# Products with the moving operand and the output taken backwards, and weights that begin 16 bytes further with each chunk

## The chip, the cores and the metric

The kernel runs on one core of one Trainium2 chip. The metric is the device time of one execution in microseconds. The matrix engine is called PE, its weight loads PEld, VectorE is DVE, ScalarE is ACT, GpSimd is POOL and SyncE is SP.

## The reference, cut to what matters

Two transformer blocks are computed one after the other on 256 tokens of 1,024 features (the first block also has 16 meta tokens, so that some of its products have 272 columns). All weights and inputs are float32.

```python
def first_block(...):
    h = concatenate([pad, meta, x])
    h = h + 0.5 * swiglu(rms_norm(h, ffn1_norm), ffn1_w_in, ffn1_w_out)   # 1024 -> 2 x 2816 -> 1024
    h = h + token_mixer(rms_norm(h, mix_norm), ...)                       # two attentions, gates, w_out
    h = h + 0.5 * swiglu(rms_norm(h, ffn2_norm), ffn2_w_in, ffn2_w_out)
    return h[:, BLOCK:]

def second_block(...):
    h = x + head_group_mixer(rmsnorm(x), ...)            # convolution and retention
    h = h + memory_cross_attention(rmsnorm(h), mem_n, ...)
    h = h + sq_relu_mlp(rmsnorm(h), up_w, down_w)        # 1024 -> 4096 -> 1024
    return rmsnorm(h)
```

Nearly all of the arithmetic is in the products of the activations with the weight matrices.

## The kernel before, in words

The activations stand feature-major: features on the 128 partitions, tokens along the free axis. The residual stream is `hA` and then `hB`, eight tiles of 128 features each. All weights are read once, in the order of their use, as a stream of chunks of up to 2,048 columns by 128 rows (`_plan`). `_Weights.load` brings a chunk into `raw` with a DMA of SP; `_high` lets ACT copy it, rounded to float32r, into `hi`; `piece` lets DVE put the rest, `raw - hi`, into `lo`. `raw`, `hi` and `lo` have three buffers each.

An activation is split in the same way into two float32r parts: `XH` and `XL` for the residual stream, `AHf`/`ALf` (feed-forward with a gate), `AHm`/`ALm` (last layer), `YH`/`YL`, `OFH`/`OFL`, `OS`, `CH`/`CL`, `OXH`/`OXL` and, for the memory, `MH`/`ML`, which take the place of `hA` and `BM`.

A product of a 128x128 block of weights with a tile of activations is then three matrix products in `mm3` (L501 to L504): high with high, high with low, low with high. Each loads its 128 columns of weights anew and takes 256 or 272 columns of the activation as the moving operand; all products of an output tile add up in one bank of PSUM (`ps` or `po`). For some output tiles the 272 columns are taken as two runs of 128 with the meta tokens left out (`qv`). `products_t` (L984 to L996) does the same for 512 output columns with the activation as the loaded operand and the weights as the moving one; it doesn't go through `mm3`.

The order of the work is written out by hand. `step` emits the products of a unit, then the work that follows the unit before it, then splits weights ahead. Nothing in the order of the work is touched by the change, except that four tiles of the mixers (`OFH`, `OFL`, `dec`, `krz`) are allocated earlier in their pools.

Tiles are placed in the order of their allocation, one behind the other: in `base` come `par`, `c0`, `cst`, `hA` (8 x 288 columns), `hB` (8 x 256), `XH` and `XL` (8 x 288 each), `BM` (8 x 290), `cosr`, `sinr` and small buffers; then the chunks' `raw`, `hi` and `lo`; then the pools of the layers. A column of float32 or float32r takes 4 bytes.

Of the kernel before, what the change touches and what calls it, by code (L numbers as in the profile page):

```python
# [17 lines left out]
P = 128  # L18
# [5 lines left out]
TP = 288  # L24
DFF = 2816
# [13 lines left out]
# ---------------------------------------------------------------- weight order  # L39
def _plan():  # L40
    """The order in which the weights are streamed: chunks of blocks
    (key, array, row tile, first column, columns)."""
# [79 lines left out]
    # ends[c]: the column behind the products that start in chunk c or, where  # L122
    # those of one output tile go on in the next chunk, behind that one
# [9 lines left out]
# ------------------------------------------------------- constants of the shapes  # L133
# [4 lines left out]
for _n, _w in (("id", P), ("bd", P), ("centre", P), ("ones512", P), ("swap", P), ("fmask", TP), ("vmask", 512)):  # L138
    _CST[_n] = (_CST_N, _w)
    _CST_N += _w  # L140
_OH_N = 384 + 272
# [70 lines left out]
def _pack(inp):  # L212
    """Layout only: transposes, permutes and concatenates the inputs."""
# [56 lines left out]
# -------------------------------------------------------------------- the stream  # L270
class _Weights:
    """Streams the weights through SBUF and splits each chunk exactly into two
    float32r parts, some columns ahead of the products that use it."""
# [27 lines left out]

    def _high(self, n):
        c, a = self.c, self.o
        at, size = self.start[c]
        if a == 0:
            self.hi[c] = self.pool.tile([P, CH], F32R, tag="hi", bufs=3, name=f"hi{c}")
            self.lo[c] = self.pool.tile([P, CH], F32R, tag="lo", bufs=3, name=f"lo{c}")
        b = min(a + n, size)
        self.nc.scalar.activation(self.hi[c][:, a:b], self.raw[c][:, a:b], AF.Copy)  # L309
        self.begun.append((c, a, b))  # L310
        self.c, self.o = (c + 1, 0) if b == size else (c, b)

    def piece(self, to, n=1024):
        """Splits a piece of the stream unless the split has come to column
        `to`; the high part runs a piece ahead of the low part."""
        if to is None or self.done >= to or self.done >= self.total:
            return False
        while sum(self.start[self.free]) <= self.used:
            self.free += 1
        while len(self.begun) < 2 and self.c < min(len(self.start), self.free + 3):  # L320
            self._high(n)
        c, a, b = self.begun.pop(0)
        if self.beside:
            self.beside((b - a) / 1024)
        self.nc.vector.tensor_tensor(self.lo[c][:, a:b], self.raw[c][:, a:b], self.hi[c][:, a:b].bitcast(F32),  # L325
                                     op=ALU.subtract)
        self.done = self.start[c][0] + b
        if b == self.start[c][1]:
            self.load()
        return True  # L330
# [5 lines left out]
    def span(self, key, to):  # L336
        """Of the products from `key` to `to`: the column behind them, and how
        far the split is to be while they run."""
# [17 lines left out]
class _Core:  # L356
    """What the phases share: the engines, the constants, the weight stream and
    the order of emission.  Work that follows a unit of products is a generator;
    at each yield a piece of the weights ahead is split, and at `yield LATER` the
    rest is put behind the next unit's products."""  # L360
# [28 lines left out]
    def step(self, key, mm, evac=(), hook=None, bg=1, last=False, to=None,  # L389
             ahead=True):  # L390
        """One unit of the weight stream: its products, then the work that
        follows the unit before it, then the split of weights ahead."""
# [25 lines left out]
def _program(ctx, tc, I, out, probe=None):  # L418
# [18 lines left out]
    def bank():  # L437
        """A bank of PSUM; those kept for long sums take part while `spare`."""
        turn[0] = (turn[0] + 1) % 8
        if spare[0] and turn[0] >= 5:  # L440
            return bank_o()
        return psum.tile([P, 512], F32, tag="ps", bufs=5, name=name("ps"))
# [3 lines left out]

    def tmp(pool, tag, n=TP, bufs=2, dt=F32):
        return pool.tile([P, n], dt, tag=tag, bufs=bufs, name=name(tag))
# [5 lines left out]
    # ------------------------------------------------ first loads  # L454
    par = base.tile([P, _PAR_N], F32, name="par")
    c0 = base.tile([P, _CST0_N], F32, name="c0")
    cst = base.tile([P, _CST_N], F32, name="cst")
    hA = base.tile([P, KD, TP], F32, tag="hA", name="hA")
    hB = base.tile([P, KD, SEQ], F32, name="hB")
    XH = base.tile([P, KD, TP], F32R, name="XH")  # L460
    XL = base.tile([P, KD, TP], F32R, name="XL")
    BM = base.tile([P, H, 290], F32, tag="BM", name="BM")
# [24 lines left out]
    def qv(ap):  # L487
        return ap.rearrange("p (s c) -> p s c", c=144)[:, :, :P]
# [4 lines left out]
    def backwards(ap):  # L493
        """The last axis, of P columns, backwards."""
# [5 lines left out]
    # ------------------------------------------------ pieces  # L500
    def mm3(o, w, x, start, stop):  # L501
        T.matmul(o, w[0], x[0], start=start, stop=False)  # L502
        T.matmul(o, w[0], x[1], start=False, stop=False)  # L503
        T.matmul(o, w[1], x[0], start=False, stop=stop)  # L504
# [13 lines left out]
    def squares(acc, src, m, n):  # L518
        """The square on ScalarE; returns what adds it to the sum."""
# [7 lines left out]
    def finish(hm, m, n, gain, acc, hold=None):  # L527
        """A tile of the residual stream is there: the parts that the next
        products take, with the next norm's gain, and the sum of squares, which
        can be put off with `hold`."""  # L530
# [11 lines left out]
    def rsqrt(dst, src):  # L542
        """dst = (src + eps) ** -0.5 as exp(-ln / 2)."""
# [4 lines left out]
    def rms(acc, n):  # L548
        """The row factor of a norm, the same on all partitions."""
# [15 lines left out]
    def products(tag, ms, x, evac, ks=range(KD), late=2, out=None, between=(), **kw):  # L565
        """Output tiles `ms` together: the last `late` input tiles come last, for
        all of them; evac(m, bank) follows.  between[i] is emitted behind the
        first part of tile i."""
# [15 lines left out]
    # ------------------------------------------------ feed-forward with a gate  # L584
    def ffn(f, d, n, h, gain, acc_in, acc_out, bg, together):
        with tc.tile_pool(name="ffn" + f, bufs=2, reuse_waits="tile") as pool:
            AH = pool.tile([P, MF, n], F32R, bufs=1, name="AH" + f)
            AL = pool.tile([P, MF, n], F32R, bufs=1, name="AL" + f)
# [49 lines left out]
    # ------------------------------------------------ token mixer  # L638
    def attention_head(pool, st, h, s_of, mask_of, cut):
        """The two query tiles of a head: scores, softmax, transposed rows,  # L640
        values.  Scores and mask come with the sign changed."""
# [54 lines left out]
    def attention_end(pool, st, OH, OL):  # L696
        """The meta tokens' part, of all heads at once."""
# [15 lines left out]
    def mixer(acc_in, acc_out):  # L713
        with tc.tile_pool(name="mixer", bufs=1, reuse_waits="tile") as pool:
            kz = pool.tile([P, H, T1], F32, tag="kz", name="kz")
            qz = pool.tile([P, H, SEQ], F32, tag="qz", name="qz")
            ks = pool.tile([P, 2, T1 + 1], F32, name="ks")
# [29 lines left out]
            def head_norm(x, n):  # L747
                """The squares' mean over the 64 features of each of a tile's two
                heads; what is yielded last turns it into 1 / rms."""
# [90 lines left out]
            def value(ps, dst, meta):  # L840
                """A tile of values, token-major; of the meta tokens a copy for
                each head."""
# [53 lines left out]
            OFH = pool.tile([P, 4, SEQ], F32R, name="OFH")  # L896
            OFL = pool.tile([P, 4, SEQ], F32R, name="OFL")
# [71 lines left out]
    # ------------------------------------------------ convolution and retention  # L969
# [14 lines left out]
    def products_t(tag, j, x, evac, **kw):  # L984
        """512 output columns, token-major."""
# [14 lines left out]
    def mixer2(acc_in, acc_out, MH, ML, accm, kx, vx, rm, held):  # L1000
        with tc.tile_pool(name="mixer2", bufs=1, reuse_waits="tile") as pool:
            U = pool.tile([P, 4, 30 + SEQ], F32, name="U")
            cv = pool.tile([P, 4, SEQ], F32, name="cv")
            dec = pool.tile([P, H, 384], F32, tag="dec", name="dec")
            krz = pool.tile([P, H, SEQ], F32, tag="krz", name="krz")
# [21 lines left out]
            def convolve(n):  # L1027
                """Some taps on VectorE, of two tiles in turn."""
# [100 lines left out]
            def row_factor():  # L1129
                """The norm's factor by token, on the partitions."""  # L1130
# [25 lines left out]
            # retention, with the decay as a full matrix  # L1156
# [37 lines left out]
            # group norm over each head's features  # L1194
# [32 lines left out]
            # layer norm over the channels of the convolution, while the other  # L1227
            # half of the output products runs
# [53 lines left out]
    # ------------------------------------------------ attention to the memory  # L1282
# [104 lines left out]
    # ------------------------------------------------ squared-relu layer and the last norm  # L1387
# [51 lines left out]
    # ------------------------------------------------ tables that depend on small inputs  # L1439
    def bias_strips(pool):  # L1440
        """The windowed attention's bias by distance, as a row per query; a tile's
        queries stand there, and in its scores, backwards."""
# [32 lines left out]
    def angles(pool):  # L1475
        """Cosines and sines of the rotary positions; the angles are reduced with
        2 pi in three parts and the multiple in two, so that products are exact."""
# [46 lines left out]
    # ------------------------------------------------ the whole  # L1524
# [70 lines left out]
```

## Time and profile before

| | us |
|---|---|
| median of 2 runs | 989.56 |
| lowest and highest | 989.34, 989.77 |
| span of the profiled execution | 988.1 |
| PE busy in it | 971.6 |
| DVE busy | 675.5 |
| ACT busy | 537.5 |

The span reaches from the first to the last instruction of one further, profiled execution; the runs' times also hold what lies around it. Busy time counts a stretch once, however many products overlap in it.

### The profile page before, as it was taken

To read this page: it belongs to the slowest core of one execution; us is meant where nothing else is said; L and a number is where in the kernel's file an instruction comes from. 1 tells how busy PE (TensorE), PEld (TensorE's weight loads), DVE (VectorE), ACT (ScalarE), POOL (GpSimd) and SP (SyncE) were. 2 spreads that over 40 slices of the span, in tenths; PEclk is the share of its full clock that TensorE was granted. 3 is DMA by queue.
4 is the path that set the end of the run, shared out by engine and by line. 5 is a ranking of instruction groups with operands and counts; after the bars stand their busy time and mean duration, and the time that the engine had idled before them with its cause. 6 is when DMAs were issued, how large, how long until landed. Compare 5 with 4: busy or idle time off the path is not lost.

```text
span 988.1 us, 18399 instructions
## 1 busy us (share of the span) xinstructions
PE 971.6 (98%) x7667; PEld 942.0 (95%) x7667; DVE 675.5 (68%) x1232; ACT 537.5 (54%) x927; POOL 9.9 (1%) x15
## 2 busy tenths in 40 slices
PE   7999999999999999999999999999999999999996
PEld 7999999999989899999999999889899999999996
DVE  5676556657885758677665657999976677665452
ACT  7545435447575656656454447556474566564441
POOL 0000000020000000000000000000000000000000
PEclk9999999999999999999999999999999999999998
DMA  8754527544433225555545656443543246564531
GB/s 299 225 219 175 171 88 235 186 163 162 160 101 126 94 100 213 214 209 176 194 164 169 201 183 240 167 150 135 208 166 139 89 175 226 193 209 177 175 124 43
DMA packets 31363, 169.05 MB, mean 171 GB/s; under 512 B 5144, under 2 KB 8864, under 8 KB 14640
## 3 DMA queue, kind: packets, MB, share of 16 engines
q1 hardware_dynamic: 30928, 167.34, 48.8%
q8 instruction: 60, 0.98, 0.4%
q10 hardware_dynamic: 288, 0.52, 0.1%
q14 instruction: 23, 0.19, 0.1%
q0 software_dynamic: 64, 0.01, 0.0%
HBM read 166.79 MB, written 1.07 MB: 170 GB/s over the span
## 4 chain that ended last, share of the span: by engine, by line
PE 96%; DMA 1%; DVE 1%; ACT 1%; SPq 0%; issue 0%; DVEq 0%; ACTq 0%
PE ps L502 18%; PE ps L503 18%; PE ps L504 18%; PE po L503 10%; PE po L502 10%; PE po L504 10%; PE ps L649 1%; DMA raw<-in_ws_dram 1%; PE ps L996 1%; PE ps L995 1%; PE ps L994 1%; PE po L691 1%; PE ps L1297 1%; PE ps L1163 0%; PE po L1335 0%; PE po L705 0%
## 5 line engine op out<-in xcount | busy, mean ns | idle before, releaser
L325 DVE TENSOR_TENSOR lo<-raw,hi 128x1024 fp32r<-128x1024 f32 (+2 forms) x334 | 373.2, 1129 | 50.7 <-ACT hi L309 45.6
L309 ACT ACTIVATE hi<-raw 128x1024 fp32r<-128x1024 f32 (+2 forms) x334 | 321.8, 978 | 142.6 <-issue 48.0
L502 PE MATMUL ps<-XH,hi 128*128 128x256 f32 (+2 forms) x976 | 283.6, 291 | 5.8 <-ACT hi L309 4.2
L504 PE MATMUL ps<-XH,lo 128*128 128x256 f32 (+2 forms) x976 | 277.0, 284 | 0.7 <-DVE lo L325 0.7
L503 PE MATMUL ps<-XL,hi 128*128 128x256 f32 (+2 forms) x976 | 276.9, 284 | 0.0
L502 PEld LDWEIGHTS ps<-XH,hi 128*128 128x128 f32 (+1 forms) x976 | 184.4, 189 | 8.4 <-ACT hi L309 4.2
L503 PEld LDWEIGHTS ps<-XL,hi 128*128 128x128 f32 (+1 forms) x976 | 184.9, 189 | 1.8 <-DVE XL L516 0.5
L504 PEld LDWEIGHTS ps<-XH,lo 128*128 128x128 f32 (+1 forms) x976 | 184.1, 189 | 1.3 <-DVE lo L325 0.9
L502 PE MATMUL po<-XH,hi 128*128 128x256 f32 (+1 forms) x456 | 129.8, 285 | 0.2 <-DVE br L1060 0.2
L504 PE MATMUL po<-XH,lo 128*128 128x256 f32 (+1 forms) x456 | 128.5, 282 | 0.5 <-DVE lo L325 0.5
L503 PE MATMUL po<-XL,hi 128*128 128x256 f32 (+1 forms) x456 | 128.4, 282 | 0.0
L502 PEld LDWEIGHTS po<-XH,hi 128*128 128x128 f32 x456 | 85.7, 188 | 0.6 <-DVE br L1060 0.4
L503 PEld LDWEIGHTS po<-XL,hi 128*128 128x128 f32 x456 | 86.0, 189 | 0.1
L504 PEld LDWEIGHTS po<-XH,lo 128*128 128x128 f32 x456 | 85.5, 187 | 0.7 <-DVE lo L325 0.7
L613 ACT ACTIVATE s<-gr 128x272 f32<-128x272 f32 (+1 forms) x44 | 18.7, 425 | 109.1 <-DVE gr L611 109.1
L502 PE MATMUL ps<-AHf,hi 128*128 128x272 f32 (+1 forms) x220 | 62.8, 286 | 0.0
L504 PE MATMUL ps<-AHf,lo 128*128 128x272 f32 (+1 forms) x220 | 62.8, 285 | 0.0
L503 PE MATMUL ps<-ALf,hi 128*128 128x272 f32 (+1 forms) x220 | 62.7, 285 | 0.0
L1034 DVE SCALAR_TENSOR_TENSOR cv<-U,par,cv 128x256 f32<-128x256 f32 x120 | 50.0, 473 | 0.2 <-ACT cv L1067 0.2
L611 DVE TENSOR_TENSOR gr<-ps,r 128x272 f32<-128x272 f32 (+1 forms) x28 | 12.1, 433 | 52.9 <-PE ps L504 45.6
L503 PE MATMUL ps<-ALm,hi 128*128 128x256 f32 x160 | 45.3, 283 | 0.0
L504 PE MATMUL ps<-AHm,lo 128*128 128x256 f32 x160 | 45.3, 283 | 0.0
(385 smaller groups left out, 1835.7 us busy)
## 6 DMA issues: line engine op xcount, KB each, us to landing
raw<-in_ws_dram SPq DMA_DIRECT2D x128, 1024.0 KB, 4.9
raw<-in_ws_dram SPq DMA_DIRECT2D x32, 704.0 KB, 4.2
raw<-in_ws_dram SPq DMA_DIRECT2D x3, 512.0 KB, 5.2
dec<-in_dec_dram SPq DMA_DIRECT2D x1, 1536.0 KB, 6.3
BM<-drow SPq DMA_DIRECT2D x2, 512.0 KB, 7.5
memraw<-in_mt_dram SPq DMA_DIRECT2D x1, 1024.0 KB, 6.9
hA<-in_xt_dram SPq DMA_DIRECT2D x3, 273.0 KB, 5.6
raw<-in_ws_dram SPq DMA_DIRECT2D x3, 256.0 KB, 5.7
```

The lines of the kernel that those rows point to most:

```text
L309: self.nc.scalar.activation(self.hi[c][:, a:b], self.raw[c][:, a:b], AF.Copy)
L325: self.nc.vector.tensor_tensor(self.lo[c][:, a:b], self.raw[c][:, a:b], self.hi[c][:, a:b].bitcast(F32), op=ALU.subtract)
L502: T.matmul(o, w[0], x[0], start=start, stop=False)
L503: T.matmul(o, w[0], x[1], start=False, stop=False)
L504: T.matmul(o, w[1], x[0], start=False, stop=stop)
L611: V.tensor_tensor(gr, g[:, :n], r[0][:, :n], op=ALU.mult)
L613: S.activation(s, gr, AF.Silu)
L649: T.matmul(ps[:, at : at + n], lhs, rhs, start=True, stop=True)
L691: T.matmul(o, st["v"](h, 0), pt[:, :SEQ], start=t % 2 == 0, stop=False)
L994: T.matmul(ps[i], xh[:, t], wh, start=k == 0, stop=False)
L995: T.matmul(ps[i], xl[:, t], wh, start=False, stop=False)
L1034: V.scalar_tensor_tensor(cv[:, m], U[:, m, j : j + SEQ], prm("cw", m * 31 + j), cv[:, m], op0=ALU.mult, op1=ALU.add)
```

## The change

`mm3` takes its two moving operands and its output with a step of -1 along each free axis, so that the last column goes first; column for column the same product is computed. The parts `hi` and `lo` of chunk c begin `place(c)` = 4 * (c % 16) columns, that is 16 * (c % 16) bytes, behind the start of their buffers, which are 64 columns longer. The other tiles of `base` are rounded up to multiples of 64 columns (256 bytes), the rows of `XH` and `XL` from 288 to 320 columns and those of `AHf` and `ALf` from 272 to 320. Four tiles of the mixers are allocated earlier, and the scratch of the dynamic DMAs is set to 4,096. Comments and docstrings are dropped.

```diff
+XP = 320
+LINE = 64
...
+def place(c):
+    return 4 * (c % 16)
...
+    def _part(self, tag, c):
+        t = self.pool.tile([P, CH + LINE], F32R, tag=tag, bufs=3, name=f"{tag}{c}")
+        at = place(c)
+        return t[:, at : at + CH]
+
     def _high(self, n):
...
-            self.hi[c] = self.pool.tile([P, CH], F32R, tag="hi", bufs=3, name=f"hi{c}")
-            self.lo[c] = self.pool.tile([P, CH], F32R, tag="lo", bufs=3, name=f"lo{c}")
+            self.hi[c] = self._part("hi", c)
+            self.lo[c] = self._part("lo", c)
...
     def tmp(pool, tag, n=TP, bufs=2, dt=F32):
-        return pool.tile([P, n], dt, tag=tag, bufs=bufs, name=name(tag))
+        t = pool.tile([P, -(-n // LINE) * LINE if pool is base else n], dt, tag=tag, bufs=bufs, name=name(tag))
+        return t[:, :n]
...
-    par = base.tile([P, _PAR_N], F32, name="par")
-    c0 = base.tile([P, _CST0_N], F32, name="c0")
-    cst = base.tile([P, _CST_N], F32, name="cst")
+    par = base.tile([P, 256], F32, name="par")[:, :_PAR_N]
+    c0 = base.tile([P, 192], F32, name="c0")[:, :_CST0_N]
+    cst = base.tile([P, _CST_P], F32, name="cst")[:, :_CST_N]
...
-    XH = base.tile([P, KD, TP], F32R, name="XH")
-    XL = base.tile([P, KD, TP], F32R, name="XL")
-    BM = base.tile([P, H, 290], F32, tag="BM", name="BM")
+    XH = base.tile([P, KD, XP], F32R, name="XH")
+    XL = base.tile([P, KD, XP], F32R, name="XL")
+    BM = base.tile([P, 2368], F32, tag="BM", name="BM")[:, : H * 290].rearrange("p (h n) -> p h n", h=H)
...
+    def turned(ap):
+        return ap[:, ::-1] if len(ap.shape) == 2 else ap[:, ::-1, ::-1]
+
     def mm3(o, w, x, start, stop):
-        T.matmul(o, w[0], x[0], start=start, stop=False)
-        T.matmul(o, w[0], x[1], start=False, stop=False)
-        T.matmul(o, w[1], x[0], start=False, stop=stop)
+        o, xh, xl = turned(o), turned(x[0]), turned(x[1])
+        T.matmul(o, w[0], xh, start=start, stop=False)
+        T.matmul(o, w[0], xl, start=False, stop=False)
+        T.matmul(o, w[1], xh, start=False, stop=stop)
...
-            AH = pool.tile([P, MF, n], F32R, bufs=1, name="AH" + f)
-            AL = pool.tile([P, MF, n], F32R, bufs=1, name="AL" + f)
+            AH = pool.tile([P, MF, -(-n // LINE) * LINE], F32R, bufs=1, name="AH" + f)[:, :, :n]
+            AL = pool.tile([P, MF, -(-n // LINE) * LINE], F32R, bufs=1, name="AL" + f)[:, :, :n]
```

## Rows read from the trace of the kernel before

**Rows 1.** The page's first part: span, then busy us (share) xinstructions.

```profile
span 988.1 us, 18399 instructions
...
PE 971.6 (98%) x7667; PEld 942.0 (95%) x7667; DVE 675.5 (68%) x1232; ACT 537.5 (54%) x927; POOL 9.9 (1%) x15
```

**Rows 2.** The page's chain that ended last, by engine and by line.

```profile
PE 96%; DMA 1%; DVE 1%; ACT 1%; SPq 0%; issue 0%; DVEq 0%; ACTq 0%
PE ps L502 18%; PE ps L503 18%; PE ps L504 18%; PE po L503 10%; PE po L502 10%; PE po L504 10%; PE ps L649 1%; DMA raw<-in_ws_dram 1%; PE ps L996 1%; PE ps L995 1%; PE ps L994 1%; PE po L691 1%; PE ps L1297 1%; PE ps L1163 0%; PE po L1335 0%; PE po L705 0%
```

**Rows 3.** Groups by shape, PE: busy us, mean ns of one | idle before.

```profile
L503 PE MATMUL ps<-XL,hi 128*128 128x256 f32 x688 | 192.2, 279 | 0.0
...
L502 PE MATMUL ps<-XH,hi 128*128 128x272 f32 x280 | 83.8, 299 | 5.8 <-ACT hi L309 4.2 <-ACT XH L510 1.6
...
L503 PE MATMUL ps<-ALm,hi 128*128 128x256 f32 x160 | 45.3, 283 | 0.0
...
L503 PE MATMUL ps<-ALf,hi 128*128 128x272 f32 x110 | 31.6, 287 | 0.0
...
L503 PE MATMUL ps<-ALf,hi 128*128 128x256 f32 x110 | 31.1, 283 | 0.0
...
L503 PE MATMUL ps<-ML,hi 128*128 128x256 f32 x64 | 17.7, 276 | 0.0
...
L995 PE MATMUL ps<-hi,ML 128*128 128x512 f32 x32 | 12.5, 392 | 0.0
...
L503 PE MATMUL ps<-YL,hi 128*128 128x256 f32 x40 | 11.3, 282 | 0.0
...
L503 PE MATMUL ps<-CL,hi 128*128 128x256 f32 x32 | 9.0, 281 | 0.0
...
L503 PE MATMUL ps<-XL,hi 128*8 128x272 f32 x8 | 2.3, 287 | 0.0
```

**Rows 4.** The same view of the weight loads, PEld.

```profile
L503 PEld LDWEIGHTS ps<-ALm,hi 128*128 128x128 f32 x160 | 30.7, 192 | 0.0
...
L503 PEld LDWEIGHTS ps<-ML,hi 128*128 128x128 f32 x64 | 12.0, 188 | 0.5 <-issue 0.5
...
L503 PEld LDWEIGHTS ps<-XL,hi 128*8 128x8 f32 x8 | 0.7, 89 | 0.4
```

**Rows 5.** Timeline in the products of the memory's keys: start us, us, instruction.

```profile
678.03 0.28 PE L503 MATMUL ps<-ML,hi 128*128 128x256 f32 x1
678.14 0.28 PE L504 MATMUL ps<-MH,lo 128*128 128x256 f32 x1
678.15 0.19 PEld L502 LDWEIGHTS ps<-MH,hi 128*128 128x128 f32 x1
...
678.94 0.28 PE L502 MATMUL ps<-MH,hi 128*128 128x256 f32 x1
```

**Rows 6.** Timeline in the last layer's second half.

```profile
957.75 0.28 PE L503 MATMUL po<-ALm,hi 128*128 128x256 f32 x1
...
957.87 0.28 PE L504 MATMUL po<-AHm,lo 128*128 128x256 f32 x1
957.87 0.19 PEld L502 LDWEIGHTS po<-AHm,hi 128*128 128x128 f32 x1
...
958.71 0.28 PE L502 MATMUL po<-AHm,hi 128*128 128x256 f32 x1
```

**Rows 7.** Groups by shape, DVE: the factor of the gates, forwards and backwards.

```profile
L801 DVE TENSOR_TENSOR hB<-ps,r 128x256 f32<-128x256 f32 x8 | 3.4, 423 | 6.7 <-PE ps L504 6.6
L801 DVE TENSOR_TENSOR gb<-ps,r 128x256 f32<-128x256 f32 x8 | 3.4, 422 | 7.4 <-PE ps L504 7.4
```

**Rows 8.** Busy time in two stretches: us, PE busy (x), PEclk, DMA share, GB/s.

```profile
880.00:960.00 80.00, 80.00 (x670) 1.00 0.49 174
80.00:180.00 100.00, 100.00 (x802) 1.00 0.50 169
```

**Rows 9.** The page's costliest groups: the low parts of the weights.

```profile
L325 DVE TENSOR_TENSOR lo<-raw,hi 128x1024 fp32r<-128x1024 f32 (+2 forms) x334 | 373.2, 1129 | 50.7 <-ACT hi L309 45.6
```

More of the change, by code (lines that the diff above doesn't have):

```diff
@@ L140 @@
     _CST_N += _w
+_CST_P = -(-_CST_N // 64) * 64
 _OH_N = 384 + 272
@@ L487, in qv @@
     def qv(ap):
-        return ap.rearrange("p (s c) -> p s c", c=144)[:, :, :P]
+        return ap[:, :TP].rearrange("p (s c) -> p s c", c=144)[:, :, :P]
     def c2(ap):
@@ L716, in mixer @@
             qz = pool.tile([P, H, SEQ], F32, tag="qz", name="qz")
+            OFH = pool.tile([P, 4, SEQ], F32R, name="OFH")
+            OFL = pool.tile([P, 4, SEQ], F32R, name="OFL")
             ks = pool.tile([P, 2, T1 + 1], F32, name="ks")
@@ L895, in mixer @@
             fmask = kc("fmask")
-            OFH = pool.tile([P, 4, SEQ], F32R, name="OFH")
-            OFL = pool.tile([P, 4, SEQ], F32R, name="OFL")
             heads = []
@@ L1001, in mixer2 @@
         with tc.tile_pool(name="mixer2", bufs=1, reuse_waits="tile") as pool:
+            dec = pool.tile([P, H, 384], F32, tag="dec", name="dec")
+            krz = pool.tile([P, H, SEQ], F32, tag="krz", name="krz")
             U = pool.tile([P, 4, 30 + SEQ], F32, name="U")
             cv = pool.tile([P, 4, SEQ], F32, name="cv")
-            dec = pool.tile([P, H, 384], F32, tag="dec", name="dec")
-            krz = pool.tile([P, H, SEQ], F32, tag="krz", name="krz")
             rq = pool.tile([P, 2, SEQ], F32, name="rqT")
@@ L1585 @@
     arrays = _pack(inputs)
-    nc = bacc.Bacc("TRN2", target_bir_lowering=False, num_devices=1)
+    nc = bacc.Bacc("TRN2", target_bir_lowering=False, num_devices=1, dynamic_dma_scratch_size=4096)
     I = {k: nc.dram_tensor(f"in_{k}_dram", v.shape, mybir.dt.from_np(v.dtype), kind="ExternalInput").ap()
```

## The prediction

> **What bounds the kernel now.** The first part of the page comes first: the span is 988.1 us and the matrix engine (PE) is busy for 971.6 us of it [rows 1]. The chain that ended last says the same in another way: 96% of it is PE, and its six largest members are the three lines of `mm3` (L502 to L504) on `ps` and `po` [rows 2]. So the other engines matter only through the 16.5 us in which PE stands still (988.1 - 971.6), and a change to how a product is taken is a change to the bound itself.
>
> A busy PE is not yet a fast PE, so the next question is how far apart the products start. In a quiet stretch of the last layer, eight starts take 957.75 to 958.71 us, 120 ns each [rows 6]; in the products of the memory keys, eight take 678.03 to 678.94, 114 ns each [rows 5]. Both are 128x256 products with a fresh 128-column weight load each, and the granted clock is 1.00 in both long stretches that I read, the higher of its two levels, 2.4 GHz [rows 8]. The mean duration of one product shows the same distance for every tile: 276 ns with `ML`, 279 with `XL`, 281 to 283 with `CL`, `YL`, `ALf` and `ALm` [rows 3]. Duration and spacing differ by a constant (283 - 120 and 276 - 114, both 162 to 163 ns), so a duration can be read as a spacing.
>
> What differs between those tiles is only where they lie. Adding up the tile sizes in the order of allocation, everything in `base` up to `BM` starts at one distance from a multiple of 256 bytes, and everything behind `BM`, whose rows of 9,280 bytes are 64 more than such a multiple, 64 bytes further. So `ALm` and the weight parts `hi` and `lo` start alike, and `MH`, which takes the place of `hA`, starts 64 bytes before them. `XH` has rows of 1,152 bytes, and its tiles lie alternately 64 before and 64 behind. The products therefore seem to feel the distance between the moving operand and the weights within 256 bytes, by up to 7 ns of 120. No run here isolates that, and one row speaks against it: the 272-wide products of `fa`, beside a load of 8 columns, take 287 ns, as long as those of `ALf` beside 128 [rows 3].
>
> **The change part by part.** No instruction is added or removed, and no wait. There are 7,080 products in `mm3` by the code's loops: 1,848 with 272 columns (both layers of the first feed-forward, and `ka`, `fa`, `va`, `kb`, `vb`) and 5,232 with 256. The 144 products of `products_t`, 512 columns wide, keep their direction.
>
> *Direction.* Neither operand is longer backwards, and each column of the result lands where it did, so evacuations are untouched. The trace has no backward matrix product. Its nearest row is on VectorE: L801 reads PSUM and `r` backwards for `gb` and forwards for `hB`, both eight times 128x256, at 422 and 423 ns [rows 7]. That prices the turn itself at nothing. What it does to the meeting of the two read streams has to be bounded. The weight stream takes (188 - 89) / 120 = 0.83 ns a column [rows 4], the moving stream, from the 512-wide product with `ML` against the 256-wide one, (392 - 276) / 256 = 0.45 ns [rows 3]: the moving operand is about twice as fast, and each weight load runs beside the product before it.
>
> If every product came to the best spacing that the trace shows, the 256-wide ones would come to a duration of 276. I take the excess as 3.5 ns for the 2,976 with `XH` and `XL` (279 and more), 7 ns for the 1,488 with `AHm`, `AHf` and `OXH` and their low parts, 5 ns for the 576 with `YH`, `CH`, `OFH`, `OS` and theirs, and nothing for the 192 with `MH`: 10.4 + 10.4 + 2.9 = 23.7 us, which also puts their mean spacing now at 114 + 23.7 us / 5,232 = 118 ns. The 272-wide ones now start 100 us / (802 - 2) = 125 ns apart [rows 8] (of those counted, 2 only reach into the stretch), and 16 columns more than 114 would be 114 + 16 x 0.45 = 121: 4 ns x 1,848 = 7.4 us. Together -31 us. There is a further bound below: a weight load of 128 columns needs 128 x 0.83 = 106 ns, so 256-wide starts can't come closer than that, (118 - 106) x 5,232 = -63 us. I take none of that.
>
> On the other side, if every product came to the worst forward spacing: 7 ns x 5,232 - 23.7 = 12.9 us for the 256-wide, and for the 272-wide from the 287 of `ALf` to the 299 of `XH` at L502 [rows 3], part of which is waiting, so not the whole: 5 ns x 1,848 = 9.2 us. Together +22 us.
>
> *The step of 16 bytes and the rounding.* With `XH` padded to 1,280 bytes a row and all long-lived tiles rounded to 64 columns, every moving tile starts alike, and the distance to the weights is set by the chunk's number alone: 16 distances, each for one chunk in 16. That replaces four distances (0, -64, +64, -32 bytes) by an even spread, and an average of fast and slow distances is about what the trace has: 118 ns lies between 114 and 120. Alone I price it at nothing, with -31 and +22 us as the ends, since eight of the sixteen are odd multiples of 16 bytes, which no tile has now.
>
> The rest is free: `dec`, `krz`, `OFH` and `OFL` are allocated earlier, but their first writes stand where they stood in each queue; the padding is never read; the smaller scratch serves Pool's two small DMAs of `cr`. ACT and DVE write the parts at 16-byte steps with the same shapes; they are busy 54% and 68% [rows 1], so a few per cent more on them would be hidden, and where that cover is gone, a tenth more on the 45.6 us in which DVE waits for `hi` [rows 9] would cost 5 us.
>
> A rule of the Trainium skill bears on both edits. The products with `ML` and `ALm` show that place matters, 276 against 283 ns [rows 3]. The Trainium skill, "TensorE: Matmul & The Clock Gate", Part 2, says that PE has two independent read ports, one for the streaming operand and one for weights, and that a load doesn't take read bandwidth from the running product. By that rule neither direction nor distance would do anything, and the time would stay at 989.6; the 7 ns in the rows speak against taking it whole.
>
> *Sum.* I take a third to a half of the -31 us, because the mean over sixteen distances can't sit at the best one everywhere and the row of `fa` leaves the cause in doubt: about -13 us. The profiled span of 988.1 lies 1.5 us below the median of the two runs, 989.6, and that remainder stays; 988.1 - 13 + 1.5 = 976.6, called 977.
>
> **The rivals.**
>
> *Fewer meetings everywhere.* If the weight load walks its columns from the last to the first, the two streams now run against each other and would afterwards run the same way, so they would meet less often at nearly any distance. For it: the best tile shows that 114 is reachable beside a full weight load [rows 5]. Against: the distance matters already, which two opposite streams should hardly feel. The whole -31 us then: 958.
>
> *The moving operand held behind the weights.* In the same direction the faster stream (0.45 ns a column) runs up behind the slower (0.83) and, where it wants the same part of the memory, can be held to its pace instead of crossing it in one step. Four columns at the slower pace cost 4 x (0.83 - 0.45) = 1.5 ns; held for 16 columns, a quarter of what lies in 256 bytes, it is 6.1 ns, x 7,080 = +43 us: 1033. It decides against the kernel from 20 / 7,080 = 2.8 ns a product, about 8 columns. For it: the stalls that the trace shows are of that size. Against: nothing shows that a stream waits for more than one step.
>
> *Backward columns written or read one by one.* If the engine joins neighbouring columns only in rising order, a product goes at a fraction of its rate. At half the rate, 0.45 x 256 = 116 ns more a product, +820 us: about 1,810. Against it is VectorE's row, where a backward read of PSUM takes the same 422 ns [rows 7], but that is another engine and a read, not a write. The Trainium skill, "SBUF — State Buffer", Door 1, has a rule on this side: PSUM's lines hold two fp32 values, and "any non-contiguous PSUM access pattern significantly slows down matmuls". Whether a step of -1 counts as such no run here shows; the time that it gives is the one just named.
>
> That the change does nothing at all lies inside the forecast's own range.
>
> **How the numbers follow.** My forecast has 0.42, fewer meetings 0.28, held behind the weights 0.20, one by one 0.10. The forecast's own range, from two thirds of the gain to two thirds of the loss, is 969 to 1004. The stated range takes in the first rival and the second with a little on either side, 948 to 1045, and leaves out the third and a tenth of the rest. Two per cent, which is about what a measurement here can tell from no change, is 970 to 1009. Faster than that: nearly all of the first rival and a little of the forecast, 0.33. Slower: the second rival, the third and none of the forecast, less the milder part of the second, 0.27. Between: 0.40.
>
> **What would show it.** In the profile after, the mean duration of the 256-wide products should come near 278 to 280 for every tile alike, with `ALm` below its 283 and `ML` above its 276, and single products in one stage should differ from chunk to chunk. All at 276 or less is the first rival; 285 to 290 the second, with the weight loads at their 188 to 192; some 390 the third. If `ALm` stays at 283 in all chunks, the distance was not the cause. The forecast would also be wrong if odd multiples of 16 bytes behave unlike the even ones that I know.

## The result, and the profile after

The changed kernel takes 994.58 us (median of two runs, 994.12 to 995.03) against 989.56: 1.0051 times the time before, with an interval of 1.0033 to 1.0069. It is slower by 5.0 us. That is a quarter of two per cent, but clear of the noise (the interval leaves out 1), and it is the other way from the forecast of 977.

The page's first part of the kernel after, and the head of its chain, answer to [rows 1, 2]:

```profile
span 992.4 us, 18428 instructions
...
PE 976.5 (98%) x7667; PEld 946.5 (95%) x7667; DVE 676.1 (68%) x1232; ACT 537.3 (54%) x927; POOL 9.9 (1%) x15
...
PE 96%; DVE 1%; DMA 1%; ACT 1%; SPq 0%; issue 0%; DVEq 0%; ACTq 0%
```

The number of matrix instructions is the same, 7,667. The span grew by 4.3 us (992.4 - 988.1) and PE's busy time by 4.9 (976.5 - 971.6), while PE stands still for 15.9 us where it was 16.5. So no new wait was made: the products themselves became slower. DVE and ACT are within 0.6 us of before.

The groups by shape show it by tile (busy us, mean ns of one | idle before), and answer to [rows 3]:

```profile
L524 PE MATMUL ps<-XL,hi 128*128 128x256 f32 x688 | 193.7, 282 | 0.0
...
L524 PE MATMUL ps<-ALm,hi 128*128 128x256 f32 x160 | 45.1, 282 | 0.0
...
L524 PE MATMUL ps<-ALf,hi 128*128 128x272 f32 x110 | 31.8, 289 | 0.0
L524 PE MATMUL ps<-ALf,hi 128*128 128x256 f32 x110 | 31.0, 281 | 0.0
...
L524 PE MATMUL ps<-ML,hi 128*128 128x256 f32 x64 | 18.1, 282 | 0.0
...
L524 PE MATMUL ps<-YL,hi 128*128 128x256 f32 x40 | 11.2, 281 | 0.0
...
L524 PE MATMUL ps<-CL,hi 128*128 128x256 f32 x32 | 9.0, 280 | 0.0
```

Before, these 256-wide tiles ran from 276 to 283 ns; now they all lie between 280 and 282. `ALm` and the 256-wide `ALf` became quicker by 1 to 2 ns, `ML` slower by 6, `XL` by 3, and `XL` is the largest group. The spread went, as it should, but to the level of the slow tiles and not to the middle.

The timeline of the memory's keys (start us, us, instruction) answers to [rows 5], where eight starts took 114 ns each:

```profile
683.11 0.28 PE L523 MATMUL ps<-MH,hi 128*128 128x256 f32 x1
683.23 0.28 PE L524 MATMUL ps<-ML,hi 128*128 128x256 f32 x1
683.35 0.28 PE L525 MATMUL ps<-MH,lo 128*128 128x256 f32 x1
...
684.07 0.28 PE L525 MATMUL ps<-MH,lo 128*128 128x256 f32 x1
```

From 683.11 to 684.07 there are eight steps, 120 ns each. The two stretches of [rows 8] (us, PE busy (x), PEclk, DMA share, GB/s) read:

```profile
880.00:960.00 80.00, 80.00 (x678) 1.00 0.52 185
80.00:180.00 100.00, 100.00 (x799) 1.00 0.49 168
```

In the last layer, where `ALm` stood at 120 ns, the products are now a little closer (678 in 80 us against 670); in the 272-wide stretch a little further apart (799 against 802). Taken over all products from the starts in the two traces, the mean distance between two starts went from 117.7 to 118.6 ns for 256 columns and from 125.1 to 125.5 for 272: 0.9 x 5,232 + 0.4 x 1,848 = 5.4 us, which accounts for the 5.0 measured. The weight loads stay at some 190 ns (those for `ALm` went from 192 to 188), and what the other engines do did not change ([rows 4, 7, 9] before):

```profile
L524 PEld LDWEIGHTS ps<-ALm,hi 128*128 128x128 f32 x160 | 30.1, 188 | 0.0
...
L824 DVE TENSOR_TENSOR hB<-ps,r 128x256 f32<-128x256 f32 x8 | 3.4, 424 | 6.9 <-PE ps L525 6.8
...
L339 DVE TENSOR_TENSOR lo<-raw,hi 128x1024 fp32r<-128x1024 f32 (+2 forms) x334 | 373.5, 1130 | 49.5 <-ACT hi L323 47.0
```

### The profile page after: what moved, and what is told of

Read it like the earlier page. It is cut to its first block, busy times and chain, and to the rows that moved or that the text cites. A ratio compares the mean times of both kernels' runs of the same rounds, so it can differ in the third digit from the quotient of the medians.

```text
span 992.4 us, 18428 instructions
## 1 busy us (share of the span) xinstructions
PE 976.5 (98%) x7667; PEld 946.5 (95%) x7667; DVE 676.1 (68%) x1232; ACT 537.3 (54%) x927; POOL 9.9 (1%) x15
## 4 chain that ended last, share of the span: by engine, by line
PE 96%; DVE 1%; DMA 1%; ACT 1%; SPq 0%; issue 0%; DVEq 0%; ACTq 0%
PE ps L523 18%; PE ps L525 18%; PE ps L524 18%; PE po L525 10%; PE po L523 10%; PE po L524 10%; PE ps L670 1%; DMA raw<-in_ws_dram 1%; PE ps L1016 1%; PE ps L1015 1%; PE ps L1017 1%; PE po L712 1%; PE ps L1318 1%; PE ps L1184 0%; PE po L726 0%; PE po L1356 0%
## 5 line engine op out<-in xcount | busy, mean ns | idle before, releaser
L339 DVE TENSOR_TENSOR lo<-raw,hi 128x1024 fp32r<-128x1024 f32 (+2 forms) x334 | 373.5, 1130 | 49.5 <-ACT hi L323 47.0
```

## The experiments

Below, "distance" is the address of the weights' first column less that of the moving operand's lowest column, in bytes modulo 256, from the tile addresses of each compiled kernel. The weights are those loaded beside the product, which are the next product's. The time from each product's start to the next is paired with that distance. The tables hold the 256-wide products whose columns lie in one run.

### Each edit alone, and one distance for all

The step of 16 bytes without the turn (the rounding and the earlier tiles stay in it):

```diff
 def mm3(o, w, x, start, stop):
-    o, xh, xl = turned(o), turned(x[0]), turned(x[1])
+    xh, xl = x
```

> The changed kernel with the columns taken forwards again; the step of 16 bytes per chunk and the rounding stay. Theory 'distance' (the spacing of products is set by the distance, within 256 bytes, between the moving operand and the weights that are loaded beside it; direction only mirrors that): spacing differs from chunk to chunk between 113 and 123 ns, its mean over the sixteen distances is near 118, time 989 to 996 us. Theory 'own place' (the moving tile's place within 256 bytes alone sets it, the weights' place does nothing): one and the same spacing in all chunks of a layer. Theory 'direction costs' (a backward product costs about 1 ns more, the step nothing): about 5 us below the changed kernel, 989 to 990 us.

Measured: 993.06 us, 1.0042 [1.0027, 1.0057].

The turn without the step, in the kernel before:

```diff
 def mm3(o, w, x, start, stop):
+    o, xh, xl = (t[:, ::-1] if len(t.shape) == 2 else t[:, ::-1, ::-1] for t in (o, x[0], x[1]))
```

> The kernel before with the columns taken backwards, nothing else changed. Theory 'distance': ALm, at distance 0, falls from 283 ns to between 280 and 282, ML, with weights 64 bytes further on, rises from 276 to 280 or 281; time 990 to 996 us. Theory 'direction costs': every tile rises by about 1 ns, ALm to 284, ML to 277; 994 to 995 us. Theory 'own place': the same order of tiles as before, ML lowest.

Measured: 992.47 us, 1.0032 [1.0020, 1.0043]. `ALm` fell from 283 to 282 ns and `ML` rose from 276 to 280, as 'distance' expected; 'direction costs' wanted both to rise by 1:

```profile
L504 PE MATMUL ps<-ALm,hi 128*128 128x256 f32 x160 | 45.0, 282 | 0.0
...
L504 PE MATMUL ps<-ML,hi 128*128 128x256 f32 x64 | 17.9, 280 | 0.0
```

Forwards, with every chunk at the same place, 64 bytes in, and then 0:

```diff
 def place(c):
-    return 4 * (c % 16)
+    return 16
```

> The changed kernel with the columns forwards and all chunks 64 bytes behind the start of their buffers, so that the weights lie 64 bytes further than every moving tile, as they did for ML. Theory 'distance': 276 to 277 ns for every 256-wide tile, 4 ns less than the mean before, x 5,232 = 21 us, and some us from the 272-wide: 962 to 970 us. Theory 'own place': the same time as with distance 0, within 2 us. Theory 'direction costs': 989 to 990 us.

Measured: 983.90 us, 0.9947 [0.9932, 0.9961]. That is a gain, but 14 us short of the range that 'distance' expected, and `ML` itself, at the distance that it had before, took 280 ns in place of 276; the last experiments take this up:

```profile
L524 PE MATMUL ps<-ML,hi 128*128 128x256 f32 x64 | 17.9, 280 | 0.0
```

> The changed kernel with the columns forwards and all chunks at the start of their buffers, so that weights and moving tiles start alike, as for ALm before. Theory 'distance': 283 ns for every 256-wide tile, 2.3 ns above the mean before, +12 us: 998 to 1004 us. Theory 'own place': the same time as with 64 bytes, within 2 us. Theory 'direction costs': 989 to 990 us.

Measured: 1000.47 us, 1.0114 [1.0099, 1.0129].

All but the kernel at 64 bytes came within the ranges of 'distance'. Each edit is a loss by itself, and together they lose 0.51%, less than the 0.74% of the two added (the intervals just leave room for the sum). The last two kernels differ in one number and lie 16.6 us apart, so where the weights lie is a cause, not a companion. 'Own place' is out, since the moving tiles lie alike in both. The weights' place alone is not enough either: in the kernel before all weights start alike, and its tiles differ. The groups by shape of the kernel at 0:

```profile
L524 PE MATMUL ps<-ALm,hi 128*128 128x256 f32 x160 | 45.3, 283 | 0.0
...
L524 PE MATMUL ps<-ML,hi 128*128 128x256 f32 x64 | 18.1, 283 | 0.0
...
L524 PE MATMUL ps<-YL,hi 128*128 128x256 f32 x40 | 11.3, 283 | 0.0
...
L524 PE MATMUL ps<-CL,hi 128*128 128x256 f32 x32 | 9.0, 283 | 0.0
```

Every tile is now as slow as `ALm` was [rows 3], `ML` too, which had been the best. A tile's speed was never its own.

The mean distance of two starts in ns, by distance:

```
bytes             0     16     32     48     64     80     96    112
before        119.9      -  118.3      -  115.2      -      -      -
turned alone  118.3      -  117.8      -  117.7      -      -      -
step alone    119.8  118.3  118.4  119.4  113.5  118.7  118.3  119.8
after         118.5  119.2  117.8  120.0  117.8  117.8  117.8  118.3

bytes           128    144    160    176    192    208    224    240
before            -      -      -      -  117.8      -      -      -
turned alone      -      -      -      -  119.0      -      -      -
step alone    118.6  119.7  119.9  118.1  115.4  116.8  116.7  119.4
after         119.9  117.9  117.8  119.9  120.0  117.8  117.9  118.7
```

Forwards the map has one deep place at 64, a shallower one at 192, and is 117 to 120 elsewhere. It is a map of means: 64 has 115.2 in one kernel and 113.5 in another, 192 has 117.8 and 115.4, so the distance alone does not settle the spacing. Before, 1,591 of the 4,604 products stood at 64, so the kernel drew on the deep place for a third of them; with the step only one chunk in sixteen does (225 products). That is the loss of the step. Backwards no distance comes below 117.7: the turn adds 2.5 ns to each of the 1,591 at 64 (+3.9 us) and 1.2 to the 1,184 at 192 (+1.4), and takes 1.6 off the 1,642 at 0 (-2.6): +2.7 us, of the 3.2 measured. With the step there is less left at 64 to lose, and the turn costs only the difference between 1.0042 and 1.0051, which the intervals don't separate.

### Is a good distance merely moved by the turn?

The changed kernel with `place` at the constant 16 columns, so that it differs from the forwards kernel at 64 by the turn alone.

> The changed kernel (columns backwards) with all chunks 64 bytes behind the start of their buffers. Theory 'best distance lost' (forwards one distance lets the 256-wide products start 113 to 114 ns apart, backwards no distance does): 117 to 118 ns for every 256-wide tile in all stretches, time 987 to 991 us. Theory 'direction only mirrors' (backwards another distance is as good, this one is as good or bad as any): anything between 113 and 120 ns, the same in all stretches. Against both, 'entry' (a run of products keeps the spacing that it was entered with) expects stretches of 113 to 114 beside stretches of 118, as forwards, and 981 to 986 us.

Measured: 989.52 us, 1.0002 [0.9993, 1.0012], 5.6 us over the forwards one. All its long 256-wide stretches run at 117.8 ns, in a repeating 115, 118, 120. Together with the row "after" of the table, which visits all sixteen distances and has nothing below 117.8, this rules out that the turn mirrors the map.

### Which half of the turn costs

The same kernel with only the moving operand turned, and with only the output turned; the columns of the results then lie mirrored.

```diff
-    o, xh, xl = turned(o), turned(x[0]), turned(x[1])
+    xh, xl = turned(x[0]), turned(x[1])
```

> The turned kernel at the constant 64 bytes (989.5), but the output of each product is written forwards, so its columns come out mirrored; same instructions and sizes. 'The order of reading' (a backward moving operand meets the weights' reads in another order, and loses the spacing of 113 ns): no stretch below 117 ns, 987 to 991. 'The order of writing' (backward writes of the output cost it): stretches at 113 ns come back as in the forwards run at 64 bytes, 981 to 986.

Measured: 990.99 us, 1.0017 [1.0008, 1.0027].

```diff
-    o, xh, xl = turned(o), turned(x[0]), turned(x[1])
+    o, (xh, xl) = turned(o), x
```

> The turned kernel at the constant 64 bytes, but the moving operand is read forwards and only the output is written backwards, so its columns come out mirrored. 'The order of reading': as the forwards run at 64 bytes, 981 to 986, with stretches at 113 ns. 'The order of writing': 987 to 991, none below 117 ns.

Measured: 983.38 us, 0.9943 [0.9928, 0.9958].

Both came as 'the order of reading' expected. At this distance writing backwards costs nothing: the second kernel is level with the forwards one at 64 bytes (983.90). Reading backwards costs all of it. One stretch of windows, 16 us in the products with `YH` (us, PE busy (x), PEclk, DMA share, GB/s), from the kernel with the moving operand turned:

```profile
382.00:398.00 16.00, 16.00 (x136) 1.00 0.45 178
```

and from the one with the output turned:

```profile
382.00:398.00 16.00, 16.00 (x144) 1.00 0.56 198
```

That is 16 us / 134 = 119 and 16 us / 142 = 113 ns to a start (of those counted, 2 only reach in).

### Do the weights' reads take part?

The kernel before, with the second product of three reduced to the first 32 outputs, so that its load takes 32 columns; the rest of that product is left out.

```diff
-        T.matmul(o, w[0], x[1], start=False, stop=False)
+        T.matmul(o[: min(32, o.shape[0])], w[0][:, : min(32, o.shape[0])], x[1], start=False, stop=False)
```

> The kernel before with the second of the three products (high weights with low activations) taken for the first 32 output features alone: it loads 32 columns of weights in place of 128 and leaves the rest of that product out. Theory 'weights' reads are the other party': the first product of each three, beside which the narrow load now runs, gets shorter, from 283 ns for AHm to 276 or less, the second and third stay. Theory 'not the weights' reads' (the 8-column loads of fa, beside which the products took as long as ever): all three stay at 283.

Measured, in one run: 987.02 us beside 989.08. Neither expectation came: all three products of a block with `AHm` and `ALm` went from 283 to 281 ns. The groups by shape, two products and a load:

```profile
L503 PE MATMUL ps<-ALm,hi 128*32 128x256 f32 x160 | 45.0, 281 | 0.0
...
L503 PE MATMUL ps<-ML,hi 128*32 128x256 f32 x64 | 17.7, 277 | 0.0
```

```profile
L503 PEld LDWEIGHTS ps<-XL,hi 128*32 128x32 f32 x968 | 105.9, 109 | 1.4 <-DVE XL L516 0.5
```

The load, at 188 to 192 ns before [rows 4], fell to 109, and the time hardly moved, but the map did: distance 0 fell from 119.9 to 117.8 ns, and 64 rose from 115.2 to 116.9. So the loads take part at distance 0. At 64 the rise lies with `XH`, `XL` and `YH`; the products with `MH` and `ML`, at 64 too, stayed at 113 to 114, so that the rise can as well be a change between the two spacings of the next section. The time of one run is too little to call; that the stall is not simply a sum over loaded columns is all that it shows.

### One distance, two spacings

At 64 bytes forwards the products keep either of two spacings for long stretches. The timeline of that kernel (the one with `place` at 16), in the products with `YH` and in the last layer:

```profile
389.74 0.28 PE L524 MATMUL ps<-YL,hi 128*128 128x256 f32 x1
...
390.54 0.28 PE L525 MATMUL ps<-YH,lo 128*128 128x256 f32 x1
...
949.79 0.28 PE L523 MATMUL po<-AHm,hi 128*128 128x256 f32 x1
...
950.50 0.28 PE L523 MATMUL po<-AHm,hi 128*128 128x256 f32 x1
```

Seven starts in 0.80 us are 114 ns each, six in 0.71 us are 118. The distance is the same, and so are the shapes. The slow spacing holds from 411 to 590 us and from 800 us to the end of the last layer, the quick one from 356 to 411 us and from 713 to 738. Of the 256-wide products in stretches of nine and more, three quarters had the slow one (3,442 of 4,581), and 3,442 x 4.5 ns = 15 us is about what this kernel lacks to the range expected of it. The run with the step had only the quick one at 64, where the chunk before stood at 48 and the one before that at 32. So an occasional chunk at another distance was tried, first at 48 bytes:

```diff
 def place(c):
-    return 16
+    return 16 if c % 6 else 12
```

> The changed kernel with the columns forwards and the chunks 64 bytes behind the start of their buffers, but every sixth at 48 bytes. Theory 'entry' (a run of products at distance 64 keeps the spacing that it was entered with, 113.3 or 117.8 ns, and coming from a chunk at 48 it is entered at 113.3): five chunks of six at 113 to 114 ns, the sixth at about 119, mean 114.4, so 2.6 ns x 5,232 = 14 us below the run with 64 alone: 968 to 973 us. Theory 'no memory' (the stretch decides): as with 64 alone, and a sixth of the products 2 ns worse, 984 to 987 us.

Measured: 979.81 us, 0.9900 [0.9883, 0.9916], between the two expectations. Then with 32 bytes in one chunk of eight, `16 if c % 8 else 8`:

> Columns forwards, chunks begin 64 bytes in, every eighth chunk 32 bytes in. 'Entry' (the 114 ns spacing at 64 bytes is entered whenever the chunk before it stood at another distance than 48, as in the forwards run with the step): 256-wide products at 64 bytes all at 113 to 114 ns, mean 114.0 outside the two-run products against 115.6 in the run with 48 bytes, so some 7 us less than that run's 979.8: 971 to 975. 'Chance of the break' (the spacing is chosen by the first products behind a pause and a chunk at 32 bytes doesn't change it): the up and down stage stays at 118 ns, 979 to 983.

Measured: 976.29 us, 0.9871 [0.9856, 0.9886]. And with 32 and then 48 in two of eight, `(8, 12, 16, 16, 16, 16, 16, 16)[c % 8]`:

> As the one before, but of eight chunks one at 32 bytes, the next at 48, six at 64: the last three steps of the forwards run with the step. 'Entry' by the way 32, 48, 64: all chunks at 64 bytes at 113 to 114 ns, mean 114.7, 974 to 977; if only this way does it and not 32 to 64, the kernel before it stays at 979 or more. 'Chance of the break': 980 to 984.

Measured: 976.38 us, 0.9871 [0.9856, 0.9886].

What each way does was counted in the traces, wherever the products run from the one chunk into the next without a pause. Behind a pause, a start 200 ns or more after the one before, the stretches of nine products and more were counted:

```
chunks before the one at 64     quick at 64 (113 to 114 ns)
32, then 48                     16 of 16 (5 in the run with the step, 11 here)
32, itself behind quick at 64    8 of 9
32, itself behind slow at 64     1 of 2
48, itself behind quick at 64    8 of 8
48, itself behind slow at 64     0 of 6
behind a pause of PE            25 of 58 (the last three kernels)
```

So a pause settles anew which of the two comes, a chunk at 48 alone keeps what there was, and 32 followed by 48 always ended in the quick one. The choice behind a pause is not drawn afresh in each execution: in the kernel with 64 alone 1,463 products from 800 us on would be 6.6 us quicker in the quick spacing, and its four runs lie within 0.7 us. The length of the pause goes with it: in the five kernels that read forwards at mostly or only 64 bytes, a start 205 or 206 ns after the one before led to the quick one 11 times of 11, at 200 or 201 ns 4 times of 21. No run varies that length by itself. Windows of the last run show the passage, in the up and down products: ahead of the two chunks, behind them, and in the last layer, where two chunks in eight stand at the dearer distances:

```profile
800.00:811.00 11.00, 11.00 (x95) 1.00 0.32 105
826.00:856.00 30.00, 30.00 (x267) 1.00 0.58 200
880.00:960.00 80.00, 80.00 (x700) 1.00 0.42 147
```

That is 11 us / 93 = 118 ns, then 30 us / 265 = 113. The run with 48 in one chunk of six came out of the same pause slowly and stayed so:

```profile
880.00:960.00 80.00, 80.00 (x681) 1.00 0.43 150
```

"Entry" therefore holds for the way 32, 48. For 32 alone it is not shown: of the chunks counted only two came behind a slow stretch, one led to the quick spacing, and the kernel had its last layer quick from the pause ahead of it. That kernel came out a microsecond above its range because the products between 600 and 770 us have a pause after every two dozen or so, and the spacing is settled anew at each. The last two kernels are quicker than both the one before and the one after, by 13 and 18 us. `ALm`, at 283 ns before, in the last of them:

```profile
L524 PE MATMUL ps<-ALm,hi 128*128 128x256 f32 x160 | 44.3, 277 | 0.0
```

## Why the prediction was wrong

*What bounds the kernel* held: PE's own pace, 96% of the chain, nothing else moved.

*Distance.* The reading of the tiles held: the pace goes by the distance modulo 256 bytes, and `ALm` was slow because it stood at 0. It held with one limit. 64 bytes allow the quick spacing but do not force it: `MH` had it before, and at the same 64 bytes `ML` took 280 ns in the kernel with 64 alone. The row of `fa` that spoke against the reading is not explained; a load of 32 columns shifted the pace at distance 0, but 8 columns beside 272-wide products were not taken apart.

*The step that failed is the "Sum": "I take a third to a half of the -31 us".* Its two terms were both mis-sized, and the first had the wrong sign.

- *Direction*, from which the -13 us were to come, costs: +3.2 us alone. The bounds of -31 and +22 us said only where products could end, and no row of the trace had a backward read of PE to say which way; the forecast put the value on the side of the gain. In place of it the runs show that reading backwards has no quick spacing at any distance (117.7 to 120.0), where reading forwards has one of 113 at 64. The turn evens the map out near its slow end.
- *The step*, of which the prediction says "Alone I price it at nothing", costs +4.2 us by its ratio (0.0042 x 989.1). The rule behind it, that an even spread gives the average of fast and slow distances, was near: the step alone has 118.3 ns where 117.7 was before. But 0.6 ns x 5,232 = 3.1 us, and the deep place is one in sixteen, while a third of the kernel's products already stood on it. The rest lies in the 272-wide products (125.1 to 125.6 ns, 0.9 us).

*What was free* was free: evacuations, DVE's splits (1,130 ns against 1,129), and nothing of the 4.2 us is left for the padding.

*The rivals.* "Fewer meetings everywhere" is out: it wanted every tile at 276 or less, and the best spacing is the one that was lost. "The moving operand held behind the weights" is out at its price: it wanted 285 to 290 ns, and no 256-wide distance rose above 120.0 from start to start. But its sign is the one that came, and at 64 bytes the backward read costs 5.6 us / 7,080 = 0.8 ns a product; a holding of some two columns (0.38 ns each by the prediction) is not ruled out, as no run shows how the two reads meet. "Backward columns written or read one by one" is out: its price was 820 us. The Trainium skill, "SBUF — State Buffer", Door 1, says that non-contiguous PSUM access slows matmuls down significantly; by the kernel with the output turned alone (983.4 against 983.9 us) a step of -1 doesn't count as such. "Nothing at all", left inside the forecast's range, came nearest. The rule of two independent read ports (the Trainium skill, "TensorE: Matmul & The Clock Gate", Part 2) would have given 989.6 for every kernel here; 983.9 against 1000.5 for 64 bytes of distance contradicts it for these float32r products.

*What was to show it.* Tiles near 278 to 280, `ALm` below 283, `ML` above 276, chunks unlike each other: the pattern came as described, 2 ns too high (280 to 282); 2 ns x 5,232 are 10 us, more than the whole loss. The signs were chosen so that they tested the distance and not the direction.

What remains open is the mechanism: why two spacings are stable at one distance, what settles the choice behind a pause, and why the backward read has only one. The map is of 256-wide products beside 128-column loads. The 272-wide ones follow the distance too, 125.4 ns at 0 and 123.4 at 64 in the two kernels with one distance, but were not taken apart further.

## What to carry to other kernels

Before averaging a periodic cost by spreading it evenly, look where the kernel stands on the map now: if many of its products stand on the best places by luck, spreading loses them, and a constant distance at the best place is the change to try first. Bounds on both sides do not make the middle a forecast; a term whose sign no row shows is to be entered at zero. And a busy share of 98% hides differences in pace of 6% (113 ns against 120): they are read from the distance of starts.

## What the runs showed of the hardware

- The starts of 256-wide float32r products with a fresh 128-column load depend on where moving operand and weights lie within 256 bytes: 119.8 ns at 0, 113.5 at 64, 115.4 at 192 and 116.7 to 119.9 at the others (step alone).
- At 64 bytes there are two spacings, 113 to 114 ns and 118. Either holds for long (the slow one from 411 to 590 us, the quick one from 356 to 411); behind a pause of PE either comes (25 of 58 quick), the same in each execution as far as the times show, and chunks at 32 and then 48 bytes led to the quick one 16 times of 16.
- A moving operand read from the last column takes 117.7 to 120.0 ns at any of sixteen distances; an output written from the last column cost nothing at 64 bytes (983.4 against 983.9 us).
